# A block with two expert half-layers on one core: every other block of one stage fed as two rounded parts instead of one exact operand

## The chip, the cores and the metric

One core of a Trainium2 chip. The metric is device time in microseconds, the median of the runs shown. Engines: PE (TensorE), DVE (VectorE), ACT (ScalarE), POOL (GpSimd) and SP, which here only issues DMAs.

## The reference, cut to what matters

256 tokens of width 2048 go through an attention-and-pooling part and then through an expert layer with 16384 experts. For each token and each of 8 heads the 16 best experts are picked, and what is computed is

```
u = take(w_down, ids)                       # rows of the first expert matrix
a = gelu(einsum('cd,ced->ce', x, u)) * g    # g: the gate of each picked expert
v = take(w_up, ids)
out = einsum('ce,ced->cd', a, v)
```

Everything is float32.

## The kernel before

The kernel treats 192 tokens densely and 64 tokens sparsely. Densely means: all 16384 experts are computed for 192 tokens, in blocks of 128 experts, and a matrix of gates (zero where an expert was not picked) is multiplied onto the result. There are 128 blocks, in two halves of 64, so four stages follow each other: first expert layer of half 0, second layer of half 0, first layer of half 1, second layer of half 1. Called here down 0, up 0, down 1, up 1. Sparsely means: for the other 64 tokens the picked rows are gathered by indirect DMA and reduced on DVE, in 128 "row steps" (`sparse_step`, L1205 to L1228; 64 of the down matrix, then 64 of the up matrix) that are dealt out over the dense steps by the list `share`.

**A step** is one block. Its weights are 128 x 2048 float32, loaded by SP in two halves of 512 KB into buffers that `fill`, `take` and `give` hand out in order: five `raw` buffers, and `spare` ones where some stage has room. In down 0 the four `hi` tiles of the weight stage serve as spares, because nothing is split there. A step can use its weights in two ways:

- **exact** (all of down 0 before): PE reads the loaded buffer directly, 16 float32 matmuls of 192 columns (L354).
- **split**: ACT rounds a half block to a `hi` tile (`split_hi`, L166), DVE subtracts to get the `lo` tile (`split_lo`, L172), and PE does a pair of matmuls per 128 rows: `hi` against 384 columns (the rounded and the rest part of the activations), `lo` against 192 (`pair`, L189 and L190). The two 192-column results are added when the block is evacuated (`both_halves`: an ACT copy L194, a DVE add L195). Down 1 is done so.

**Order.** The schedule is manual: each engine's instructions stand in program order, written out by `run`. For step n it emits: the evacuation of block n-1 (`h_done`: for exact blocks an ACT gelu L1109 and an ACT copy L1111); the first 8 matmuls or pairs; one turn of the side work; the other 8; the DVE and ACT split of the second half of block n+1, if that one is split; the late DVE multiply of the evacuation (L1112); a row step, if one is due (L1213 and a POOL gather for two row steps later, L1202); another turn of the side work; and the split of the first half of block n+2, if that one is split.

**Side work in down 0** is `gate_groups`, which builds the gate matrix for 8 tokens at a time, 24 groups. A group takes three turns, so one and a half steps: eight gate matmuls on PE (L1075, called G below); then the gates go from PSUM onto what is already evacuated (DVE multiplies L1087) and into the rest (ACT copies L1089, L1090, then an ACT-issued DMA L1091), called M; then the one-hot matrices of a later group on DVE (L1056, L1059), called O. So the turns of three steps in a row are G,M / O,G / M,O. In M the ACT copies stand behind the DVE multiplies of the same tile.

Of the kernel before, what the change touches and what calls it, by code (L numbers as in the profile page):

```python
# [10 lines left out]
F32 = mybir.dt.float32  # L11
F32R = mybir.dt.float32r
U32 = mybir.dt.uint32
AF = mybir.ActivationFunctionType
# [3 lines left out]
P = 128  # L18
D = 2048
# [8 lines left out]
HB = NB // 2  # L28
SP = 64
ND = S - SP  # L30
AB = 21
RS = 24
TG = 8
HW = 1024
RAW_BUFS = 5
HL_BUFS = 4
T1_BUFS = 11
S1_BUFS = 4
KS = 9
# [54 lines left out]
def peer_block_kernel(ctx: ExitStack, tc, xT_d, c_d, cols_d, const_d, ada_d, gates_d, wide_d, blk_d, mix_d, br_d,  # L94
                      wout_d, wq_d, keys_d, down_d, up_d, rows_d, fg_d, out_d):
    nc = tc.nc
    ctx.enter_context(tc.manual_schedule())

    def ext(pool):
        return ctx.enter_context(pool)  # L100

    per = ext(tc.tile_pool(name="per", bufs=1))
    wst = ext(tc.tile_pool(name="wst", bufs=3))
# [9 lines left out]
    def psum(name):  # L113
        return psp.tile([P, 512], F32, tag="ps", name=name)
# [5 lines left out]
    spare, next_spare = [], [0]  # L120
# [23 lines left out]
    def take():  # L144
        fill()
        raw, kind = queue.popleft()
        held.append(kind)
        return raw

    def give():  # L150
        use[held.popleft()] -= 1
        fill()
# [5 lines left out]
    def split_hi(s, i):  # L158
        hw = s.w // 2
        if hw == HW:  # L160
            r = take()
        else:
            s.raw = take() if i == 0 else s.raw
            r = s.raw[:, i * hw:(i + 1) * hw]
        hi = wst.tile([P, hw], F32R, tag="hi", bufs=HL_BUFS, name="hi")
        nc.scalar.copy(hi, r)  # L166
        s.hs.append(hi)
        return r

    def split_lo(s, i, r):  # L170
        lo = wst.tile(list(r.shape), F32R, tag="lo", bufs=HL_BUFS, name="lo")
        nc.vector.tensor_sub(lo, r, s.hs[i].bitcast(F32))  # L172
        s.ls.append(lo)
        if s.w == D or i:
            give()
# [5 lines left out]
    def mm3(out, wh, wl, ah, al, start, stop):  # L181
        nc.tensor.matmul(out, wh, ah, start=start, stop=False)  # L182
        nc.tensor.matmul(out, wh, al, start=False, stop=False)  # L183
        nc.tensor.matmul(out, wl, ah, start=False, stop=stop)  # L184

    def pair(ps, wh, wl, a, start, stop):


        nc.tensor.matmul(ps[:, :2 * ND], wh, a.rearrange("p s n -> p (s n)"), start=start, stop=False)  # L189
        nc.tensor.matmul(ps[:, :ND], wl, a[:, 0, :], start=False, stop=stop)  # L190

    def both_halves(ps, out):

        nc.scalar.copy(out, ps[:, ND:2 * ND])  # L194
        nc.vector.tensor_add(out, ps[:, :ND], out)  # L195
# [10 lines left out]
    x2f = hT.rearrange("p k s -> p (k s)")[:, :KC * ND].rearrange("p (k n) -> p k n", n=ND)  # L206
# [37 lines left out]


    class Step:
        def __init__(self, src, mm, evac=None, w=D, ada=(), before=(), after=(), exact=False):
            self.exact = exact
            self.src, self.mm, self.evac, self.w = src, mm, evac, w
            self.ada, self.before, self.after = list(ada), list(before), list(after)  # L250
            self.hs, self.ls = [], []
            self.rows, self.ticks = 0, []

    steps = []
# [36 lines left out]
    def act(a):  # L291
        if a[0] == "ada":
            ada_half(a[1], a[2])
        elif a[0] == "call":
            a[1]()
        elif a[0] == "prep":
            for f in a[1].after:
                f()
        else:
            split_lo(a[1], a[2], a[3] if len(a) > 3 else split_hi(a[1], a[2]))  # L300
# [41 lines left out]
    def block_step(src, act, done, N=S, both=False, **kw):  # L342

        st = {}

        def mm(hs, ls, half):
            if half == 0:
                st["ps"] = psum("blk")
            raw = take() if kw.get("exact") else None
            for r in range(8):  # L350
                k, c = half * 8 + r, slice(r * P, (r + 1) * P)
                a = act(k)
                if raw is not None:
                    nc.tensor.matmul(st["ps"][:, :ND], raw[:, c], a, start=k == 0, stop=k == KC - 1)  # L354
                elif both:
                    pair(st["ps"], hs[half][:, c], ls[half][:, c], a, k == 0, k == KC - 1)
                else:
                    mm3(st["ps"][:, :N], hs[half][:, c], ls[half][:, c], a[:, 0, :], a[:, 1, :], k == 0, k == KC - 1)
            if raw is not None:
                give()  # L360

        return Step(src, mm, (lambda: done(st.pop("ps"))) if done else None, **kw)
# [6 lines left out]
    def tmp1(name):  # L369
        return pa.tile([P, S], F32, tag="t1", bufs=T1_BUFS, name=name)  # L370

# [324 lines left out]
    for g in range(4):  # L696
        def done(ps, g=g):
            p0 = tmp1("p0")
            nc.scalar.copy(p0, ps[:, :S])
            side2.append(pool_side(g, p0))  # L700
# [55 lines left out]
    pp = {}  # L756
# [6 lines left out]
    while gates:  # L763
        steps.append(branch_step(new.popleft() if new[0] <= have and len(new) >= len(old) else old.popleft()))
        if (len(new) + len(old)) % 2 or len(new) + len(old) < 4:
            c, g = gates.popleft()
# [250 lines left out]
    NG = ND // TG  # L1017
# [6 lines left out]
    def get_A(hs, q):  # L1024
        while len(hs["A"]) <= q:
            n = min(AB, HB - AB * len(hs["A"]))
            if n == AB:
                hs["A"].append(b16([P, NG, n, TG], F32, "A"))
            else:
                tail = hT.rearrange("p k s -> p (k s)")[:, KC * ND:KC * ND + NG * n * TG]  # L1030
                hs["A"].append(tail.rearrange("p (g n u) -> p g n u", n=n, u=TG))
        return hs["A"][q]
# [11 lines left out]
    def gate_groups():  # L1044
# [25 lines left out]
        for g in range(NG):  # L1070
# [24 lines left out]
                ohs.append(onehots(g + 2))  # L1095
            yield

    def h_done(half, bl, ps):
        hs = half_state[half]
        dst = get_A(hs, bl // AB)[:, :, bl % AB, :]  # L1100
        n = hs["g"]
        if n:
            hsum = pp["pk2"].tile([P, NG, TG], F32, tag="s1", bufs=S1_BUFS, name="hsum")
            src = hsum
            if half:
                both_halves(ps, hsum.rearrange("p g u -> p (g u)"))
            else:
                src = ps[:, :ND].rearrange("p (g u) -> p g u", u=TG)
            nc.scalar.activation(hsum, src, AF.Gelu)  # L1109
            if n < NG:  # L1110
                nc.scalar.copy(dst[:, n:], hsum[:, n:])  # L1111
            late.append(lambda: nc.vector.tensor_mul(dst[:, :n], hsum[:, :n], dst[:, :n]))  # L1112
        else:
            nc.scalar.activation(dst, ps[:, :ND].rearrange("p (g u) -> p g u", u=TG), AF.Gelu)
        hs["evac"] = bl + 1

    def room(where=None):

        spare.clear()
        if where == "h":  # L1120
            f = hT.rearrange("p k s -> p (k s)")
            spare.extend(f[:, i * HW:(i + 1) * HW] for i in range(KC * ND // HW))
        elif where:
            spare.extend(wst.tile([P, HW], F32, tag="hi", bufs=HL_BUFS, name="spare") for _ in range(HL_BUFS))

    def open_late():
        pa_ctx.close()
# [109 lines left out]
    def keep(oc):  # L1237

        pp["ctx"].close()
        pp["pf"] = ext(tc.tile_pool(name="pf", bufs=1))  # L1240
        fin["acc"] = pp["pf"].tile([P, 2, D], F32, name="acc")
        for q in range(4):
            c = slice(q * 512, (q + 1) * 512)
            evacuate(fin["acc"][:, 0, c], oc[2 * q], q)
            fold(fin["acc"][:SP, 1, c], oc[2 * q + 1])
# [26 lines left out]
    for half in range(2):  # L1272
        n0 = len(steps)
        for bl in range(HB):
            steps.append(block_step(down_d[half * HB + bl], x2act if half else lambda k: x2f[:, k, :],
                                    lambda ps, half=half, bl=bl: h_done(half, bl, ps), both=half == 1, exact=half == 0))
        if half == 0:
            for m in range(2 * KC):
                steps[n0 - 12 + m].ada.append((80 + m // 2, m % 2))
            steps[n0 + 1].ticks.append(lambda: room("split"))  # L1280
            steps[n0 + 2].ticks.append(open_late)
            steps[n0 + 5].ticks.append(lambda: side.append(gate_groups()))
            steps[n0 + 22].ticks.append(gate_row)
            steps[n0 + HB - 8].ticks.append(lambda: room())
        oc = []
        for bl in range(HB):
            steps.append(up_step(half, bl, oc))
        if half == 0:
            steps[-1].evac = lambda oc=oc: keep(oc)
# [3 lines left out]
    load_gates(n0 + 24, NA - 1, 1)  # L1293


    share = [0.95] * (HB - RS) + [0.47] * HB + [0.42] * HB + [0.55] * (HB - 4)
    total, seen = sum(share), 0.0
    for i, w in enumerate(share):
        n = int(seen / total * 2 * NP + 1e-6)
        seen += w  # L1300
        steps[n0 - 2 * HB + RS + i].rows = int(seen / total * 2 * NP + 1e-6) - n
    steps[n0 - HB + 1].ticks.append(lambda: room("h"))
    steps[n0 - 8].ticks.append(lambda: room())
    steps[n0 + 26].ticks.append(lambda: room("h"))
# [6 lines left out]
    pk, pk2 = pp["pk"], pp["pk2"]  # L1311
# [4 lines left out]
    for t in (1, 0):  # L1316
        for q in range(4):
            c = slice(q * 512, (q + 1) * 512)
            tmp = b16([P, 512], F32, "fin")
            src = oc[2 * q + t]  # L1320
            if t:
                src = fin["rows"][:, c]
# [81 lines left out]
```

## Time and profile before

| | |
|---|---|
| median of 3 runs | 2030.64 us (2026.82 to 2032.2) |
| profiled execution, its own time | 2034.78 us, of which the traced span is 2033.0 us |
| PE busy | 1977.0 us, 97% |
| DVE busy | 1662.1 us, 82% |
| ACT busy | 887.0 us, 44% |
| POOL busy | 378.5 us, 19% |
| DMA | 648.81 MB, mean 319 GB/s |

The span is longer than any busy time. The profile's chain of waits, which follows the last instruction back to what released it, runs through PE for 75% of the span, through DVE for 6%, DMA for 5%, ACT for 2%. Busy shares are means over stages of different kinds, so a stretch is read by its own rows.

### The profile page before, as it was taken

Reading aid. Unit: us, or ns where it says so; the run is one execution under the profiler, and the core shown is the slowest. Engines: PE = TensorE matmul, PEld = TensorE weight load, DVE = VectorE, ACT = ScalarE, POOL = GpSimd, SP = SyncE. Lnnn points to the kernel's source line nnn. Section 1 sums busy time; section 2 is a strip of 40 time slices with the busy share of each in tenths; the row PEclk is TensorE's granted clock in tenths of the full one; section 3 lists DMA queues with packets and bytes.
Section 4 is the critical chain, followed back from the end, with each engine's and each line's share of the span. In section 5 each row is a group of like instructions: output and inputs, shape, how many; then the busy total and the mean of one; then the engine's idle time right before and its main releaser. Section 6 shows DMA issues by size and latency. Waiting matters only on the chain.

```text
span 2033.0 us, 33021 instructions
## 1 busy us (share of the span) xinstructions
PE 1977.0 (97%) x12300; PEld 1826.7 (90%) x12300; DVE 1662.1 (82%) x2888; ACT 887.0 (44%) x1457; POOL 378.5 (19%) x384
## 2 busy tenths in 40 slices
PE   7999999999999999999999999999999999999994
PEld 5889999999999999999999888888999999888883
DVE  8787888889888978487886878888897888888886
ACT  2144554544545521012223555555555555545553
POOL 3101231102114710011111100002111112222220
PEclk8999999999999999999999999999999999999997
DMA  9996877789897788899998999998989988999992
GB/s 393 419 369 216 312 269 267 261 278 316 298 326 260 248 281 305 290 363 367 350 354 330 364 333 361 352 356 286 363 328 328 338 333 319 366 349 351 349 349 69
DMA packets 172547, 648.81 MB, mean 319 GB/s; under 512 B 21217, under 2 KB 30721, under 8 KB 155745
## 3 DMA queue, kind: packets, MB, share of 16 engines
q1 hardware_dynamic: 148144, 499.18, 68.2%
q0 software_dynamic: 19200, 136.87, 18.3%
q10 hardware_dynamic: 5042, 10.64, 1.4%
q8 instruction: 97, 1.59, 0.3%
q14 instruction: 64, 0.52, 0.1%
HBM read 636.13 MB, written 10.49 MB: 318 GB/s over the span
## 4 chain that ended last, share of the span: by engine, by line
PE 75%; DVE 6%; DMA 5%; ACT 2%; issue 2%; POOL 0%; DVEq 0%; ACTq 0%; POOLq 0%
PE blk L354 16%; PE oc L1165 12%; PE oc L1167 12%; PE blk L189 8%; PE oc L1169 6%; PE blk L183 4%; PE blk L182 4%; PE blk L184 4%; PE blk L190 4%; DMA raw<-in_blk_dram 2%; PE gps L1075 2%; DVE lo L172 2%; DMA raw<-in_down_dram 1%; DMA raw<-in_wout_dram 1%; ACT hi L166 1%
## 5 line engine op out<-in xcount | busy, mean ns | idle before, releaser
L172 DVE TENSOR_TENSOR lo<-raw,hi 128x1024 fp32r<-128x1024 f32 (+1 forms) x467 | 555.3, 1197 | 120.9 <-ACT hi L166 118.3
L166 ACT CAST hi<-raw 128x1024 fp32r<-128x1024 f32 (+1 forms) x467 | 473.3, 1020 | 387.9 <-PE oc L1165 127.1
L189 PE MATMUL blk<-xn,hi 128*128 128x384 f32 x1024 | 296.2, 363 | 2.4 <-ACT hi L166 1.7
L190 PE MATMUL blk<-xn,lo 128*128 128x192 f32 x1024 | 258.0, 252 | 1.5 <-DVE lo L172 1.5
L1202 POOL DMA_INDIRECT rows<-in_up_dram,spidx x64 | 131.6, 2055 | 494.6 <-DVE rows L1220 238.7
L354 PE MATMUL blk<-hT,raw 128*128 128x192 f32 x1280 | 212.3, 326 | 0.0
L354 PEld LDWEIGHTS blk<-hT,raw 128*128 128x128 f32 x1280 | 207.7, 190 | 0.0
L1165 PE MATMUL oc<-hi,a 128*128 128x512 f32 x512 | 202.6, 396 | 1.7 <-ACT hsum L1109 1.7
L1165 PE MATMUL oc<-lo,a 128*128 128x512 f32 x512 | 203.8, 398 | 0.0
L1167 PE MATMUL oc<-hi,a 128*128 128x512 f32 x512 | 202.7, 396 | 0.0
L1169 PE MATMUL oc<-hi,a 128*128 128x512 f32 x512 | 202.5, 395 | 0.0
L1167 PE MATMUL oc<-lo,a 128*128 128x512 f32 x512 | 201.2, 393 | 0.0
L190 PEld LDWEIGHTS blk<-xn,lo 128*128 128x128 f32 x1024 | 197.1, 193 | 2.0 <-DVE lo L172 2.0
L219 DVE SCALAR_TENSOR_TENSOR raw<-raw,cb 128x1024 f32<-128x1024 f32 x144 | 188.9, 1330 | 9.6 <-DMA raw<-in_ada_dram 7.0
L189 PEld LDWEIGHTS blk<-xn,hi 128*128 128x128 f32 x1024 | 194.0, 189 | 3.0 <-ACT hi L166 1.9
L166 ACT CAST hi<-hT 128x1024 fp32r<-128x1024 f32 x118 | 124.0, 1051 | 125.7 <-PE oc L1165 72.1
L172 DVE TENSOR_TENSOR lo<-hT,hi 128x1024 fp32r<-128x1024 f32 x118 | 142.7, 1221 | 32.6 <-ACT hi L166 32.6
L1213 DVE SCALAR_TENSOR_TENSOR rows<-rows,rows 128x2048 f32<-128x2048 f32 x64 | 146.2, 2284 | 27.9 <-DMA rows<-in_rows_dram,spidx 27.9
L1220 DVE SCALAR_TENSOR_TENSOR rows<-rows,sph,rows 128x2048 f32<-128x2048 f32 x63 | 147.7, 2344 | 1.6 <-DMA rows<-in_up_dram,spidx 1.6
L1202 POOL DMA_INDIRECT rows<-in_rows_dram,spidx x64 | 62.6, 978 | 447.0 <-DVE a L1149 233.6
L182 PE MATMUL blk<-xna,hi 128*128 128x256 f32 x480 | 138.6, 289 | 0.0
L184 PE MATMUL blk<-xna,lo 128*128 128x256 f32 x480 | 135.8, 283 | 0.0
(307 smaller groups left out, 4156.1 us busy)
## 6 DMA issues: line engine op xcount, KB each, us to landing
raw<-in_down_dram SPq DMA_DIRECT2D x181, 512.0 KB, 6.7
raw<-in_up_dram SPq DMA_DIRECT2D x165, 512.0 KB, 6.8
raw<-in_ada_dram SPq DMA_DIRECT2D x144, 512.0 KB, 5.7
hT<-in_up_dram SPq DMA_DIRECT2D x91, 512.0 KB, 7.3
raw<-in_blk_dram SPq DMA_DIRECT2D x80, 512.0 KB, 6.0
spare<-in_down_dram SPq DMA_DIRECT2D x48, 512.0 KB, 7.0
xraw<-in_ada_dram SPq DMA_DIRECT2D x36, 512.0 KB, 9.8
raw<-in_wout_dram SPq DMA_DIRECT2D x32, 512.0 KB, 5.9
```

The costliest lines, as they stand in the source:

```text
L166: nc.scalar.copy(hi, r)
L172: nc.vector.tensor_sub(lo, r, s.hs[i].bitcast(F32))
L182: nc.tensor.matmul(out, wh, ah, start=start, stop=False)
L184: nc.tensor.matmul(out, wl, ah, start=False, stop=stop)
L189: nc.tensor.matmul(ps[:, :2 * ND], wh, a.rearrange("p s n -> p (s n)"), start=start, stop=False)
L190: nc.tensor.matmul(ps[:, :ND], wl, a[:, 0, :], start=False, stop=stop)
L219: nc.vector.scalar_tensor_tensor(raw, raw, 1.0, cb[:, i * HW:(i + 1) * HW], op0=ALU.mult, op1=ALU.mult, accum_out=modp[:, i, m:m + 1])
L354: nc.tensor.matmul(st["ps"][:, :ND], raw[:, c], a, start=k == 0, stop=k == KC - 1)
L1165: nc.tensor.matmul(o, a[:, P:P + 2 * SP], w, start=st_, stop=sp_)
L1167: nc.tensor.matmul(o, a[:, :P], w, start=st_, stop=sp_)
L1169: nc.tensor.matmul(o, a[:, P + 2 * SP:], w, start=False, stop=False)
L1202: nc.gpsimd.indirect_dma_start(rows[:, j % 2, :], None, table_rows["down" if j < NP else "up"], bass.IndirectOffsetOnAxis(sp["idx"][:, j % ...
```

## The change

Down 0's blocks 26, 28, ..., 60 (18 blocks) become split blocks. Their `hi` and `lo` parts stand in two fixed tile pairs, one for each half of a block, instead of rotating tiles; two `hi` and two `lo` tiles remain as spare load buffers (before: four `hi`). The first row step moves from step 24 to step 28 (`RS`), and `share` deals the 128 row steps out anew: down 0, up 0, down 1 and up 1 get 29, 35, 29 and 35 instead of 38, 30, 26 and 34.

```diff
-RS = 24
+RS = 28
+SPLIT0 = range(26, 61, 2)
...
-        hi = wst.tile([P, hw], F32R, tag="hi", bufs=HL_BUFS, name="hi")
+        hi = pp["hi"][i] if s.fixed else wst.tile([P, hw], F32R, tag="hi", bufs=HL_BUFS, name="hi")
...
-        lo = wst.tile(list(r.shape), F32R, tag="lo", bufs=HL_BUFS, name="lo")
+        lo = pp["lo"][i] if s.fixed else wst.tile(list(r.shape), F32R, tag="lo", bufs=HL_BUFS, name="lo")
...
+    def is_split(half, bl):
+        return half == 1 or bl in SPLIT0
...
-            if half:
+            if is_split(half, bl):
                 both_halves(ps, hsum.rearrange("p g u -> p (g u)"))
...
+        elif is_split(half, bl):
+            hsum = pp["pk2"].tile([P, NG, TG], F32, tag="s1", bufs=S1_BUFS, name="hsum")
+            both_halves(ps, hsum.rearrange("p g u -> p (g u)"))
+            nc.scalar.activation(dst, hsum, AF.Gelu)
...
-            spare.extend(wst.tile([P, HW], F32, tag="hi", bufs=HL_BUFS, name="spare") for _ in range(HL_BUFS))
+            for tag in ("hi", "lo"):
+                pp[tag] = [wst.tile([P, HW], F32R, tag=tag, bufs=HL_BUFS, name=tag) for _ in range(2)]
+                spare.extend(wst.tile([P, HW], F32, tag=tag, bufs=HL_BUFS, name="spare") for _ in range(2))
...
-            steps.append(block_step(down_d[half * HB + bl], x2act if half else lambda k: x2f[:, k, :],
-                                    lambda ps, half=half, bl=bl: h_done(half, bl, ps), both=half == 1, exact=half == 0))
+            steps.append(block_step(down_d[half * HB + bl], x2act if is_split(half, bl) else lambda k: x2f[:, k, :],
+                                    lambda ps, half=half, bl=bl: h_done(half, bl, ps), both=is_split(half, bl),
+                                    exact=not is_split(half, bl), fixed=half == 0))
...
-    share = [0.95] * (HB - RS) + [0.47] * HB + [0.42] * HB + [0.55] * (HB - 4)
+    share = [0.82] * (HB - RS) + [0.55] * HB + [0.44] * HB + [0.58] * (HB - 4)
```

## Rows read from the trace of the kernel before

The columns of a stretch are: start:end, its length, then busy us of PE, PE's weight loads, DVE, ACT and POOL (instructions in brackets), granted clock, DMA share, GB/s. A timeline row is: start us, us, engine, line, instruction, and in brackets the idle time before it and what ended it.

**Rows 1.** Chain of waits, down 0: start us, us, what (x counts weight loads too).

```profile
725.54 2.60 PE blk L354 x16
...
870.32 1.78 PE gps L1075 x16
872.10 7.80 PE blk L354 x48
```

**Rows 2.** Busy time by stretch, down 0: start:end, length, busy us, clock, DMA share.

```profile
870.30:1062.00 191.70, 191.70 (x1283) 191.70 (x1282) 155.78 (x399) 41.19 (x200) 30.19 (x30) 1.00 0.97 357
```

**Rows 3.** Timeline of PE, split blocks of down 1: start, us, instruction.

```profile
1557.12 0.36 PE L189 MATMUL blk<-xn,hi 128*128 128x384 f32 x1
...
1557.41 0.36 PE L189 MATMUL blk<-xn,hi 128*128 128x384 f32 x1
```

**Rows 4.** Timeline of DVE, down 0, late: M, O, late multiply.

```profile
1062.98 0.52 DVE L1087 TENSOR_TENSOR A<-gps,A 128x84 f32<-128x84 f32 x3
1063.87 0.52 DVE L1087 TENSOR_TENSOR A<-gps,A 128x84 f32<-128x84 f32 x3 [0.37 <-PE gps L1075]
1064.31 0.68 DVE L1056 TENSOR_TENSOR o<-iota,rt 128x512 f32<-128x512 f32 x1
...
1067.56 0.33 DVE L1112 TENSOR_TENSOR A<-hsum,A 128x168 f32<-128x168 f32 x1
1067.80 2.29 DVE L1213 SCALAR_TENSOR_TENSOR rows<-rows,rows 128x2048 f32<-128x2048 f32 x1
```

**Rows 5.** Timeline of DVE, down 0, early: a row step, then M.

```profile
894.90 2.29 DVE L1213 SCALAR_TENSOR_TENSOR rows<-rows,rows 128x2048 f32<-128x2048 f32 x1 [0.34 <-DMA rows<-in_rows_dram,spidx]
...
897.12 0.59 DVE L1087 TENSOR_TENSOR A<-gps,A 128x84 f32<-128x84 f32 x4
897.63 0.68 DVE L1056 TENSOR_TENSOR o<-iota,rt 128x512 f32<-128x512 f32 x1
```

**Rows 6.** Timeline of DVE, down 1: split, add, split, multiply, split.

```profile
1419.99 0.35 DVE L195 TENSOR_TENSOR hsum<-blk,hsum 128x192 f32<-128x192 f32 x1
1420.26 1.21 DVE L172 TENSOR_TENSOR lo<-raw,hi 128x1024 fp32r<-128x1024 f32 x1
1421.39 0.35 DVE L1112 TENSOR_TENSOR A<-hsum,A 128x192 f32<-128x192 f32 x1
1421.71 1.23 DVE L172 TENSOR_TENSOR lo<-raw,hi 128x1024 fp32r<-128x1024 f32 x1
```

**Rows 7.** Timeline of ACT, down 0, early: the end of M, then an evacuation.

```profile
897.54 0.33 ACT L1089 COPY A<-gps 128x48 f32<-128x48 f32 x2 [9.92 <-DVE A L1087]
...
898.83 0.33 ACTq L1091 DMA_DIRECT2D g2d<-gst  x1
899.20 0.33 ACT L1109 ACTIVATE hsum<-blk 128x192 f32<-128x192 f32 x1 [0.40 <-PE blk L354]
899.56 0.33 ACT L1111 COPY A<-hsum 128x168 f32<-128x168 f32 x1
```

**Rows 8.** Timeline of ACT, down 1: gelu behind the DVE add, then a cast.

```profile
1420.37 0.37 ACT L1109 ACTIVATE hsum<-hsum 128x192 f32<-128x192 f32 x1 [0.94 <-DVE hsum L195]
1420.64 1.04 ACT L166 CAST hi<-raw 128x1024 fp32r<-128x1024 f32 x1
```

**Rows 9.** Timeline of ACT, down 0, late: the DMA issue that ends M.

```profile
1065.03 0.33 ACTq L1091 DMA_DIRECT2D g2d<-gst  x1
```

**Rows 10.** Waits from 870 to 1062 us: us in total, times, longest.

```profile
ACT A L1089 <- DVE A L1087: 83.5, 28, 10.3
```

**Rows 11.** Busy time by stretch: up 0, down 1, up 1, a slow stretch of down 1.

```profile
1103.00:1403.00 300.00, 298.33 (x1279) 240.06 (x1279) 242.19 (x315) 151.63 (x194) 34.10 (x31) 1.00 0.93 348
1403.00:1706.00 303.00, 299.16 (x2080) 297.99 (x2079) 257.92 (x307) 173.44 (x266) 45.25 (x27) 0.99 0.91 334
1706.00:2000.00 294.00, 294.00 (x1263) 236.99 (x1262) 248.31 (x290) 150.52 (x192) 75.62 (x32) 1.00 0.90 333
1542.00:1549.00 7.00, 6.69 (x28) 6.70 (x29) 7.00 (x10) 4.18 (x7) 1.06 (x1) 0.57 1.02 410
```

More of the change, by code (lines that the diff above doesn't have):

```diff
@@ L246, in peer_block_kernel, with __init__ @@
     class Step:
-        def __init__(self, src, mm, evac=None, w=D, ada=(), before=(), after=(), exact=False):
-            self.exact = exact
+        def __init__(self, src, mm, evac=None, w=D, ada=(), before=(), after=(), exact=False, fixed=False):
+            self.exact, self.fixed = exact, fixed
             self.src, self.mm, self.evac, self.w = src, mm, evac, w
```

## The prediction

> **What bounds the kernel now.** I read the chain of waits first, then the busy time of the stretch that is changed, then the timelines of DVE and ACT in it. The chain through down 0 is PE alone: exact blocks and G in turn [rows 1]. Between two G's lie 24 exact matmuls in 7.80 us, so a block of 16 takes 5.20; a G takes 1.78. The first G starts 144.8 us after the stage, which is block 27.5 at 5.20 plus small gaps: turn G stands between the halves of block 27, and by its number every step from 27 on is G,M (27, 30, ...), O,G (28, 31, ...) or M,O (29, 32, ...).
>
> From 870.3 to 1062 us PE is busy for all of 191.7 us, at full clock; DVE for 155.8 (81%) [rows 2]. That is five times six blocks: 38.34 us per six (6 x 5.20 + 4 x 1.78 = 38.32, so the reading fits). DMA is busy to 0.97 there but holds nothing up: no load stands in the chain. So this stage is worth what PE is worth, as long as PE is what ends last. That is what the change puts at stake, since it moves work from PE to DVE and ACT.
>
> **PE's part.** A pair for 128 rows is issued every 0.285 us (1557.12 to 1557.41) [rows 3], so a split block takes 16 x 0.285 = 4.56 us against 5.20: 0.64 saved, 11.5 us over 18 blocks, if PE never waits. Six blocks would then take 3 x 5.20 + 3 x 4.56 + 7.12 = 36.4 us.
>
> **DVE's part.** It takes its instructions in the order written, so I sum what one turn of six steps costs it, by distances from start to start where the rows allow it.
> - O: 3.25 us (1064.31 to 1067.56) [rows 4]; four in six steps, 13.0.
> - M: 0.51 early (897.12 to 897.63, four multiplies) [rows 5], and late, with six multiplies, twice 0.44 (1063.87 to 1064.31) = 0.88 [rows 4]; the 0.37 between its halves is a wait for PE that a DVE behind PE doesn't have. Four: 2.0 or 3.5.
> - the late multiply: 0.24 [rows 4]; six, 1.4.
> - a row step: 2.22 (894.90 to 897.12) [rows 5].
> - new, the `lo` of half a block: 1.13 (1420.26 to 1421.39); new, the add of a split evacuation: 0.27 [rows 6]. Six and three: 6.8 and 0.8.
>
> Without row steps that is 24.1 us early, 25.6 late. Of the new deal 26 row steps fall on steps 29 to 59, about 5.0 in six steps: 11.2 us. Together 35.3 to 36.8, as much as PE's 36.4. DVE's spare time is used up, even by its bare work.
>
> **The new waits.** DVE's `lo` needs ACT's cast, and ACT too goes in order. Three times in six steps the cast stands behind something that waits for DVE itself, and `lo` is DVE's next instruction, so DVE stands still; everything behind it (multiply, row step, O, the next `lo`) waits along, and PE for the next `lo`.
> - Step G,M with a split block (30, 36, ...): the first `lo` of block n+2 comes right after M. Step M,O with an exact block (29, 35, ...): the second `lo` of block n+1 comes right after M. ACT must first do M's copies, which wait for DVE's multiplies in the trace already (83.5 us, 28 times [rows 10]), then issue a DMA, then cast. Late: DVE is free at 1064.31, the DMA issue is at 1065.03 [rows 9], the next ACT instruction comes 0.37 after an issue (898.83 to 899.20) [rows 7], the cast takes 1.04 [rows 8], and `lo` starts 0.03 after its end (1421.68 to 1421.71 [rows 6, 8]): 1066.47, a wait of 2.16. Early: DVE free at 897.63 [rows 5], ACT free at 899.20 [rows 7], `lo` at 900.27: 2.64.
> - Step G,M with an exact block (33, 39, ...): the second `lo` comes right after the add, with only G between, and that is PE's. ACT must do the gelu that needs the add, a copy, then the cast: add at 1419.99, DVE free at 1420.26, gelu at 1420.37 [rows 6, 8]; copy 0.36 later and 0.33 long [rows 7]; cast to 1422.10, `lo` at 1422.13: 1.87.
> - The other three `lo` come after an O or a row step, which cover the cast (O,G with an exact block: 3.25 of O against 2.14).
>
> So 7.15 us of waiting early and 6.19 late. Being late does not shorten them, as each starts from DVE's own instruction. No row shows such a wait in down 0, so their bounds are zero, if something hides them, and 3 x 2.64 = 7.9. I take the worked-out values, because every link stands in a row.
>
> **The sum.** DVE is level with PE at block 29, since steps 27 and 28 carry no row step and only 3.9 and 4.6 us. From there it needs: step 29, 0.27 + 0.51 + 2.64 + 1.13 + 0.24 + 3.25 = 8.0; three early turns (steps 30 to 47) at 24.1 + 7.15 = 31.2; two late (48 to 59) at 25.6 + 6.19 = 31.7; 26 row steps, 57.7. That is 222.9 us. The last `lo` that a split block needs (the second of block 60) has 5.7 us of step 59 behind it, so it is done at 217.2, and block 60 ends half a block later, 219.5. Before, the same stretch was PE's: 5.20 + 5 x 38.34 + 6.98 (block 60 with a G) = 203.9. So block 60 ends 15.6 us later, less 1.3 for blocks 26 and 28: **14.3 us lost**. After it DVE has little to do (no O, no split) and is level again by block 63.
>
> What else moves. Nine row steps with their gathers leave down 0, 5 go to up 0, 3 to down 1, 1 to up 1. In up 0 DVE is busy 242 of 300 us [rows 11]; 5 x 2.22 makes it 253, and up 1 runs with 248 of 294 and PE busy throughout, so I take 0 there. Down 1 is closer: 258 of 303, PE idle for 3.8; three more row steps cost 0 to 6.7, I take 1. SP's loads keep their number and nine buffers, those of a split block are freed earlier, by `lo`; PE waits for no load before, the stage gets longer and nine gathers leave it: 0, with 0 to 2 us kept for the hand-over to up 0, either way. The fixed tiles make a cast wait for the matmuls of two blocks ago: long done when DVE is behind, 0, and up to half a block (2.3 us) once, before it is.
>
> By the profiled execution 2034.8 + 15.3 = 2050; it lies 4.1 above the median of the runs shown, so the forecast is **2046 us**. About 0.3% (6 us) is what a measurement of this kernel can tell from no change.
>
> **The rivals.**
> 1. *PE stays the bound* (the three waits are hidden or much shorter). DVE's bare work of 35.3 to 36.8 keeps up with 36.4, PE gains its 11.5, down 1 costs 1: 2020. For it: DVE's 81%. Against it: it leaves no room for any wait; it decides from where the waits, worked out at 36.5 us over the stage (rival 2), are under 15. The Trainium skill (Perfetto Trace Analysis, Identifying the Most-Contended Engine) has occupancy as the measure for Vector and a fair one of how close it is to its limit; by that the added 7.6 us less the row steps fit into the idle 7.2 and this rival would be the answer. The trace agrees that DVE has room now, but the rule doesn't see a wait that DVE causes itself. 0.17.
> 2. *No change.* The waits of 36.5 us in all (2.64 + 3 x 7.15 + 2 x 6.19) shrink to about 21, and the loss of 15.3 with them: 2031. For it: ACT's copies might overlap more than the rows of M show. Against it: two of the three links are single instructions with their own rows. 0.13.
> 3. *Down 1 pays too.* The three row steps there fall where DVE already ends last, 6.7 on top, 2053; with all three waits at 2.64, 3 to 5 more: 2057. For it: PE's 3.8 us of idle in down 1. Decided by whether a row step falls among its blocks 10 to 25. 0.08.
> 4. *The clock falls.* PE's new idle gaps between the halves of split blocks (up to 5 us) could bring it down, as in down 1 at 1542, where the mean of 7 us after a stall was 0.57 [rows 11]. At 1.2 GHz a block takes twice as long; an estimate from the 18 split blocks alone is 18 x 4.56 = 82, above 2110. Up 0, with 1.7 us of PE idle, keeps 1.00. The skill's rule (TensorE: Matmul & The Clock Gate, The HAM clock gate) has the throttled state as the default that activity releases; by it these gaps speak against the change. 0.02.
>
> **How the numbers follow.** The forecast has 0.60, with its own range of 2037 (the gelu wait hidden, 5 x 1.87 less) to 2054. Rivals 0.17, 0.13, 0.08, 0.02. Slower by over 0.3%: 0.60 + 0.08 + 0.02 = 0.70; within: 0.13; faster: 0.17. The range of 2025 to 2060 leaves out most of rival 1, and rival 4.
>
> **What would show it.** Right: between blocks 30 and 60 DVE stops before `lo` for ACT's cast, three times in six steps, about 2 us each, some 30 us in all; PE stops between the halves of split blocks for `lo`; split blocks still issue a pair every 0.285; DVE busy rises to about 85% and the six steps take 42 to 43 us. Wrong: PE without gaps from block 26 to 60 and a stage 11 us shorter, or DVE busy near 100% without waits for ACT.

## The result, and the profile after

| | before | after |
|---|---|---|
| median | 2030.64 us | 2048.85 us (2044.28 to 2055.03, 5 runs) |
| ratio | | 1.0078, 95% interval 1.0064 to 1.0091 |
| profiled execution | 2034.78 us | 2048.85 us, span 2047.1 us |
| DVE busy | 1662.1 us, 82% | 1710.3 us, 84% |
| down 0, first to last exact matmul | 377.3 us | 391.9 us |

The kernel is slower by 0.8% by the ratio (the two medians alone are 0.9% apart). In the profiled executions that is 14.1 us, and down 0 alone is 14.6 us longer; from the first matmul of up 0 to the end of the span it takes 0.7 us more than before (930.99 and 930.30).

Busy time by stretch, after (start:end, length, busy us of PE, its weight loads, DVE, ACT and POOL, granted clock, DMA share, GB/s): down 0 from block 27 on, a part of it, then up 0, down 1 and up 1.

```profile
868.80:1106.00 237.20, 222.16 (x1490) 217.85 (x1489) 196.54 (x472) 80.14 (x272) 30.66 (x27) 0.97 0.82 285
915.00:945.00 30.00, 27.05 (x174) 26.20 (x173) 24.36 (x54) 9.94 (x32) 3.76 (x3) 0.91 0.84 298
...
1118.00:1417.00 299.00, 295.88 (x1262) 238.02 (x1261) 253.53 (x330) 150.64 (x193) 33.72 (x36) 0.99 0.96 366
1417.00:1720.00 303.00, 301.59 (x2090) 300.41 (x2089) 262.67 (x308) 174.46 (x267) 47.17 (x28) 1.00 0.92 341
1720.00:2014.00 294.00, 294.00 (x1264) 237.02 (x1263) 253.10 (x294) 150.49 (x192) 101.17 (x34) 1.00 0.91 340
```

In down 0 PE was busy throughout [rows 2]; now it stands idle for 15 of 237 us, and DVE, at 196.5 of 237.2 (83%), isn't full either. In the three later stages PE is busy for about 99% or more, as before [rows 11]; up 0 is 3.0 us longer and down 1 2.3 us shorter. The chain of waits, close up from 950 to 970 us, says who holds the end:

```profile
951.18 1.13 DVE lo L173
952.31 0.28 DVE hsum L196
...
952.61 0.37 ACT hsum L1113
...
953.00 0.30 ACT A L1115
953.30 0.96 ACT hi L167
...
954.28 1.23 DVE lo L173
...
959.63 2.21 DVE rows L1223 x2
961.84 1.14 DVE lo L173
```

Where only PE stood [rows 1], the chain goes from DVE's add (952.31) through ACT's gelu, copy and cast back to DVE's `lo`, and then through a row step to the next `lo`. DVE's timeline there has the two kinds of wait side by side (in brackets the idle time before an instruction, and what ended it):

```profile
951.10 1.22 DVE L173 TENSOR_TENSOR lo<-raw,hi 128x1024 fp32r<-128x1024 f32 x1
952.23 0.34 DVE L196 TENSOR_TENSOR hsum<-blk,hsum 128x192 f32<-128x192 f32 x1
954.28 1.23 DVE L173 TENSOR_TENSOR lo<-spare,hi 128x1024 fp32r<-128x1024 f32 x1 [1.71 <-ACT hi L167]
...
963.16 0.23 DVE L1088 TENSOR_TENSOR A<-gps,A 128x84 f32<-128x84 f32 x1
963.99 0.54 DVE L1088 TENSOR_TENSOR A<-gps,A 128x80 f32<-128x80 f32 x3 [0.60 <-ACT A L1115]
966.98 1.22 DVE L173 TENSOR_TENSOR lo<-raw,hi 128x1024 fp32r<-128x1024 f32 x1 [2.45 <-ACT hi L167]
...
976.10 0.69 DVE L1088 TENSOR_TENSOR A<-gps,A 128x84 f32<-128x84 f32 x4
979.10 1.23 DVE L173 TENSOR_TENSOR lo<-raw,hi 128x1024 fp32r<-128x1024 f32 x1 [2.31 <-ACT hi L167]
```

and ACT's timeline shows what it did meanwhile:

```profile
952.61 0.36 ACT L1113 ACTIVATE hsum<-hsum 128x192 f32<-128x192 f32 x1 [4.31 <-DVE hsum L196]
953.00 0.30 ACT L1115 COPY A<-hsum 128x128 f32<-128x128 f32 x1
953.21 1.04 ACT L167 CAST hi<-spare 128x1024 fp32r<-128x1024 f32 x1
...
976.58 0.23 ACT L1090 COPY A<-gps 128x84 f32<-128x84 f32 x1 [9.08 <-DVE A L1088]
...
977.65 0.33 ACTq L1092 DMA_DIRECT2D g2d<-gst  x1
978.02 1.04 ACT L167 CAST hi<-raw 128x1024 fp32r<-128x1024 f32 x1 [0.40 <-ACT gst L1091]
```

At 952.23 DVE adds; ACT, idle for 4.31 us, can only then do the gelu (952.61) and the copy, and casts from 953.21 to 954.25; `lo` starts at 954.28. At 976.10 DVE multiplies; ACT, idle for 9.08, can only then copy, issue a DMA and cast to 979.06; `lo` starts at 979.10. The cast needs nothing of either; it only stands behind them in ACT's order. The waits from 855 to 1115 us (us in total, times, longest):

```profile
DVE lo L173 <- ACT hi L167: 37.4, 18, 2.6
...
PEld blk L191 <- DVE lo L173: 14.5, 13, 2.4
PE blk L191 <- DVE lo L173: 11.0, 11, 2.1
...
DVE A L1088 <- ACT A L1115: 2.8, 6, 0.6
```

Sixteen of the eighteen in the first row fall between block 29 and block 60: 33.8 us.

### The profile page after: what moved, and what is told of

It reads as the page before. It is cut to its first block, busy times and chain, and to the rows that moved or that the text cites. A ratio compares the mean times of both kernels' runs of the same rounds, so it can differ in the third digit from the quotient of the medians.

```text
span 2047.1 us, 33143 instructions
## 1 busy us (share of the span) xinstructions
PE 1977.2 (97%) x12300; PEld 1824.5 (89%) x12300; DVE 1710.3 (84%) x2942; ACT 925.9 (45%) x1511; POOL 396.5 (19%) x384
## 4 chain that ended last, share of the span: by engine, by line
PE 71%; DVE 10%; DMA 5%; ACT 3%; issue 2%; ACTq 0%; DVEq 0%; POOL 0%
PE oc L1177 12%; PE oc L1175 12%; PE blk L355 10%; PE blk L190 9%; PE oc L1179 6%; PE blk L191 4%; PE blk L184 4%; PE blk L183 4%; PE blk L185 4%; DVE lo L173 2%; DMA raw<-in_wout_dram 2%; DMA raw<-in_blk_dram 2%; ACT hi L167 1%; PE gps L1076 1%; DVE raw L220 1%
## 5 line engine op out<-in xcount | busy, mean ns | idle before, releaser
L173 DVE TENSOR_TENSOR lo<-raw,hi 128x1024 fp32r<-128x1024 f32 (+1 forms) x487 | 580.4, 1200 | 117.2 <-ACT hi L167 114.7
L167 ACT CAST hi<-raw 128x1024 fp32r<-128x1024 f32 (+1 forms) x487 | 494.3, 1021 | 380.5 <-PE oc L1175 142.1
L190 PE MATMUL blk<-xn,hi 128*128 128x384 f32 x1312 | 389.6, 368 | 4.8 <-ACT hi L167 4.1
L191 PE MATMUL blk<-xn,lo 128*128 128x192 f32 x1312 | 333.6, 254 | 11.7 <-DVE lo L173 11.7
L191 PEld LDWEIGHTS blk<-xn,lo 128*128 128x128 f32 x1312 | 253.6, 193 | 15.5 <-DVE lo L173 15.5
L190 PEld LDWEIGHTS blk<-xn,hi 128*128 128x128 f32 x1312 | 249.4, 190 | 6.0 <-ACT hi L167 4.8
L1212 POOL DMA_INDIRECT rows<-in_up_dram,spidx x64 | 150.2, 2347 | 442.5 <-DVE rows L1230 224.3
L173 DVE TENSOR_TENSOR lo<-hT,hi 128x1024 fp32r<-128x1024 f32 x118 | 143.0, 1223 | 36.2 <-ACT hi L167 36.2
L355 PE MATMUL blk<-hT,raw 128*128 128x192 f32 x960 | 160.8, 326 | 0.0
L355 PEld LDWEIGHTS blk<-hT,raw 128*128 128x128 f32 x960 | 156.1, 190 | 0.0
```

Of the source, the lines that this page charges most:

```text
L1212: nc.gpsimd.indirect_dma_start(rows[:, j % 2, :], None, table_rows["down" if j < NP else "up"], bass.IndirectOffsetOnAxis(sp["idx"][:, j % ...
```

## The experiments

The theory was that DVE's waits for casts, which DVE causes itself through ACT's order, turn PE's gain into a loss. The rivals: the fixed tiles or DVE's bare work do it (the waits only fill idle time), or the new deal of row steps, or a lower clock of PE. "Before" is the kernel before on the same chip; down 0 is the time from the first to the last start of its exact matmuls, in the profiled execution.

| kernel | median us | before | ratio (95%) | down 0, against before's 377.3 |
|---|---|---|---|---|
| after | 2048.85 | 2030.64 | 1.0078 (1.0064 to 1.0091) | +14.6 |
| first cast ahead (e3) | 2041.39 | 2033.55 | 1.0037 (1.0024 to 1.0051) | +5.7 |
| second ahead, kept (e9) | 2026.58 | 2033.45 | 0.9961 (0.9949 to 0.9974) | -1.3 |
| both ahead, kept (e8) | 2021.52 | 2033.45 | 0.9935 (0.9919 to 0.9952) | -8.7 |
| deal alone (e6) | 2031.29 | 2033.55 | 0.9992 (0.9979 to 1.0004) | +0.4 |
| every third, no wait (e4) | 2024.78 | 2033.45 | 0.9954 (0.9941 to 0.9967) | -6.8 |
| every third, a wait each (e5) | 2034.35 | 2033.45 | 1.0004 (0.999 to 1.0018) | +0.8 |
| split alone (e7) | 2075.05 | 2032.21 | 1.0198 (1.0172 to 1.0224) | +31.4 |
| both ahead, old deal (e10) | 2046.63 | 2032.21 | 1.0066 (1.0043 to 1.0089) | +12.7 |

The last column is of one execution of each kernel. Those of e9 (2032.73) and e4 (2033.7) took 6 and 9 us more than their medians, so for these two the ratio says more than the stage: e4 is 6.8 shorter in down 0 there and 5.7 longer outside of it, which was not followed up.

**Both casts ahead (e1), and the second alone (e2): two tries that tell nothing.** The cast of a first half moves ahead of the late multiply, the row step and the turn, that of a second half ahead of the evacuation. The loads are issued in the order in which the halves are now taken (that hunk is not shown).

```diff
@@ run @@
+                elif first and first[0] == "half" and first[1].fixed:
+                    parts[0][0] = first + (split_hi(first[1], first[2]),)
+                    ahead[id(first[1]), first[2]] = held.pop()
                 if steps[n - 1].evac:
...
+            for i, a in enumerate(parts[1]):
+                if a[0] == "half" and a[1].fixed:
+                    parts[1][i] = a + (split_hi(a[1], a[2]),)
             while late:
                 late.popleft()()
```

> The changed kernel, with both of ACT's casts of a split block of down 0 written earlier: the second half's ahead of the evacuation before it, the first half's ahead of the row step and of the second turn of side work. DVE's instructions and their order are the same. Theory (DVE waits for casts that stand behind its own results, 36.5 us over the stage): the waits fall under 6 us, DVE's bare work no longer ends last, PE's stage comes to its 11.5 us below the kernel before: 2020 to 2026 us. Rival (DVE's added work alone fills the stage): the work is the same, so 2044 or more. Rival (the new deal of row steps costs the time): 2044 or more.

> As e1, but only the cast of the second half of a split block is written earlier. Theory: of each six steps' three waits two go (1.7 behind the gelu, 2.2 to 2.6 behind M, and the 0.4 to 0.6 that M loses before it): about 25 us of the stage, so 2048.85 - 25 = 2024, within 5. Rivals (bare work, or the deal): 2044 or more.

They took 2052.03 us (ratio 1.0097, 1.008 to 1.0114) and 2054.59 us (1.0106, 1.0085 to 1.0126). A half that is cast ahead still needs its buffer for `lo`, but the next `take` had already handed that buffer to a later load: `lo` is made of another block's data there, and waits for that load. The waits of the first of the two:

```profile
DVE lo L176 <- DMA spare<-in_down_dram: 28.6, 5, 7.3
...
PEld blk L194 <- DVE lo L176: 20.7, 7, 6.5
```

28.6 us of a wait that the edit itself put in: neither time bears on the theory.

**The first cast alone ahead** (e3) has only the second hunk, and no buffer problem.

> As e1, but only the cast of the first half is written earlier. Theory: one wait of 2.2 to 2.6 us goes in each six steps, five in the stage, 12 us: 2037, within 4; with e2 the two add up to more than e1 gains, since e1 meets PE's own time. Rivals (bare work, or the deal): 2044 or more.

2041.39, against the ratio of after some 8 us better (0.41% of 2030.64), down 0 shorter by 8.9. On DVE the waits behind M before a first half are gone; what is left:

```profile
909.09 1.23 DVE L176 TENSOR_TENSOR lo<-raw,hi 128x1024 fp32r<-128x1024 f32 x1 [1.74 <-ACT hi L170]
...
921.74 1.23 DVE L176 TENSOR_TENSOR lo<-spare,hi 128x1024 fp32r<-128x1024 f32 x1 [2.54 <-ACT hi L170]
```

The missing ones are five of 2.11 to 2.56 in after, 11.7 us together; 8.9 of them came back. The median is 0.4 outside of what was expected.

**Both ahead, and the second alone, with the buffer kept** until its `lo` has read it (nothing is handed on while a half is held):

```diff
     def take():
-        fill()
+        if not ahead:
+            fill()
...
-    def give():
-        use[held.popleft()] -= 1
-        fill()
+    def give(key=None):
+        use[ahead.pop(key) if key in ahead else held.popleft()] -= 1
+        if not ahead:
+            fill()
```

> Both casts ahead as in e1, but no load is handed a buffer while a half that was cast ahead still stands unread in one: in e1 and e2 DVE's subtraction read a buffer that the next block's load had already been given, so that it waited for that load and the rest parts were not those of its block; their times say nothing of the theory. Theory (waits for casts behind DVE's own results): they fall under 6 us, PE ends last again, 2020 to 2027 us. Rival (DVE's bare work fills the stage by itself): 2036 or more, as e3 leaves it.

> As e8, but only the second half's cast is ahead. Theory: of the waits about 20 us (2.2 to 2.6 behind M five times, 1.7 behind the gelu five times) and 2 us inside M go, and five waits of 2.1 to 2.6 stay: 2048.85 - 22 = 2027, within 4. Rival (bare work): 2036 or more.

Both times came as expected, and the first kernel beats both the one before and the one after: 0.9935. The 2 us inside M that were expected to go with the second stayed, 3.1 in six waits in either kernel. The waits of the first (e8) between blocks 29 and 60, and its busy time there:

```profile
DVE hsum L199 <- ACT hsum L198: 10.0, 7, 1.7
...
DVE A L1098 <- ACT A L1125: 3.1, 6, 0.7
...
PEld blk L194 <- DVE lo L176: 2.8, 2, 1.6
...
DVE rows L1233 <- DMA rows<-in_rows_dram,spidx: 1.8, 2, 1.1
```
```profile
877.00:1085.00 208.00, 205.70 (x1443) 205.19 (x1442) 192.83 (x465) 80.82 (x274) 30.66 (x27) 1.00 0.90 319
```

There is no row of `lo` waiting for a cast. DVE does the same work in 208 us at 93%, and PE is busy for 99%. DVE has no free time here either: its 192.83 us of work and 15.3 of waits (10.0, 3.1, 1.8 and one of 0.4) fill the 208, so it is about level with PE, which waits for it for 2.8. The 10.0 is a remnant of the same kind: in one step of six the add waits for ACT's evacuation copy, which now stands behind M's copies and the cast put ahead of it. So the waits that DVE causes itself fell from 36.2 to some 13 us. Nothing differs from after but the place of the ACT casts and, for its sake, when buffers are handed on and the order of the loads, so the loss is shown to be those waits and what follows from them; the fixed tiles and DVE's bare work can't be it. With only the second cast ahead, the waits behind M before a first half are left:

```profile
DVE lo L176 <- ACT hi L170: 13.9, 6, 2.6
```

**The deal alone** (e6): before, with `RS` 28 and the new `share`.

> The kernel before with nothing changed but the first row step (28) and the new deal of row steps; all blocks of down 0 are exact. Theory: PE is the bound throughout and nothing it waits for has moved: 2030, within 4. Rival (the deal costs the time, in up 0 and down 1): 2040 to 2049.

No change (0.9992), and down 0 within 0.4 us. That rival falls.

**Every third block split**, 11 blocks either way, and only the turn differs:

```diff
-SPLIT0 = range(26, 61, 2)
+SPLIT0 = range(28, 61, 3)   # the other kernel: range(29, 61, 3)
```

> The changed kernel with blocks 28, 31, ..., 58 of down 0 split (11 instead of 18), nothing else changed. In these steps the first half's lo comes after O, and the second half's after a G and an exact block's evacuation, so neither cast stands behind anything that waits for DVE. Theory: no new waits; DVE needs 16.5 to 17.5 us for three steps, PE 18.5, so PE ends last and gains 11 x 0.64 = 7 us on the kernel before: 2024, within 3. Rival (bare work: 11 of 18 splits cost 11 of 18 of the 18 us): 2042.

> As e4 with blocks 29, 32, ..., 59: the same 11 splits, the same work on every engine, one step later in the turn of the side work. Now the first half's lo comes right after M each time. Theory: eleven waits of 2.1 to 2.7 us; three steps take DVE 18.9 to 19.3 us against PE's 18.5 (before: 19.2), so 2029 to 2034, 5 to 10 us above e4. Rival (bare work): the same time as e4, within 2.

Starting at 28 (e4), the first cast comes behind O and the second behind the gelu of an exact block, which doesn't wait for DVE. Starting at 29 (e5), the first comes behind M. Waits of the first, then of the second:

```profile
ACT hsum L195 <- PE blk L191: 34.8, 10, 3.9
...
DVE lo L173 <- ACT hi L167: 7.6, 4, 3.8
```
```profile
DVE lo L173 <- ACT hi L167: 25.2, 11, 2.6
...
PEld blk L191 <- DVE lo L173: 5.5, 3, 2.1
```

The first has down 0 shorter by 6.8 us, just what PE saves (11 x 0.64 = 7.0), and PE waits for no `lo`. The second has one wait per split block and loses it all again. Equal work, medians 9.6 us apart; the second is 0.35 above the time expected of it.

**The old deal**, `RS` 24 and the old `share`, with the split of after (e7), and with both casts ahead (e10):

> The changed kernel with the row steps as they were before the change: first one at step 24, and the old deal. Only the split blocks are left of the change. Theory: DVE is what ends last from block 30 to 60, so each row step there costs its full 2.2 us; the old deal has 30 of them on steps 29 to 59, the new one 26: 9 us above the changed kernel, 27 above the kernel before. Rival (PE or the clock is what ends last): the same time as the changed kernel, within 3.

> Casts ahead as in e8, with the old deal of row steps. Theory: without the waits DVE's bare work is 35 to 37 us in six steps with the new deal, beside PE's 36.4, and about 1.8 more with the old one: 37 to 39, so DVE ends last by 1 to 2 us in each of five turns: 3 to 8 us above e8, some 4 to 9 below the kernel before. If DVE had room to spare, the same as e8.

Both missed: 2075.05 where about 2059 was expected, and 14 us above before where 4 to 9 below was. Down 0 is longer than with the new deal by 16.8 and 21.4 us. The row steps from the split on, in after and in the kernel with both casts ahead and the old deal (count, shortest/median/longest ns, first and last start), the first of the latter on DVE's timeline, and the first in the kernel before:

```profile
L1223 DVE SCALAR_TENSOR_TENSOR rows<-rows,rows x27: 2280/2284/2289, 883.6 to 1102.5; 128x2048 f32<-128x2048 f32 x27
```
```profile
L1233 DVE SCALAR_TENSOR_TENSOR rows<-rows,rows x37: 2271/2282/2293, 866.0 to 1106.5; 128x2048 f32<-128x2048 f32 x37
```
```profile
865.97 2.29 DVE L1233 SCALAR_TENSOR_TENSOR rows<-rows,rows 128x2048 f32<-128x2048 f32 x1 [8.30 <-DMA rows<-in_rows_dram,spidx]
```
```profile
864.15 2.29 DVE L1213 SCALAR_TENSOR_TENSOR rows<-rows,rows 128x2048 f32<-128x2048 f32 x1 [8.21 <-DMA rows<-in_rows_dram,spidx]
```

(In after a 28th follows at 1109.35, so the difference is nine.) I had counted only the four more on steps 29 to 59. But steps 25 to 28 carry four more (by `share` the first row steps fall on steps 25 and 29, one behind `RS`; the ninth comes after step 59), and DVE's work for the first split blocks stands behind them. Eight at 2.22 each are 17.8 us, beside the 16.8 and 21.4, and neither kernel with the new deal has free time on DVE. That each costs its full time there is argued from this sum; no run shows it apart. The first also waits for its gather, 8.30 us here and 2.74 in the split alone; the kernel before has that wait too, 8.21, and there it costs nothing. How much of it DVE passes on was not tested. The span of the split alone is 41.2 us longer than before's (2074.2): 31.4 of it in down 0, 2.8 ahead of it, and 7 later, which were not followed up.

## Why the prediction was right

The forecast of 2046 stands on one reading: DVE, not PE, ends last in down 0 once blocks are split, because of waits that it causes itself. That is what the chain and the experiments show. By its steps:

- *PE saves 11.5 us if it never waits.* Split blocks issue a pair every 0.29 us in after, as in [rows 3]:

```profile
1097.98 0.36 PE L190 MATMUL blk<-xn,hi 128*128 128x384 f32 x1
...
1098.27 0.36 PE L190 MATMUL blk<-xn,hi 128*128 128x384 f32 x1
```

  With the casts ahead 8.7 of the 11.5 are there, and with every third block 6.8 of 7.0; the two pieces (5.7 and -1.3 against 14.6) make 8.9 + 15.9 = 24.8, and both together 23.3, where DVE comes level with PE (the -1.3 is of e9's long execution, so the 15.9 may be more). Rival 1 gave 2020 for this; it is the time of the kernel with both casts ahead, 2021.52.
- *A turn of six steps costs DVE 42 to 43 us.* From one M to the fourth after it, in after, with five row steps between:

```profile
1018.69 0.88 DVE L1088 TENSOR_TENSOR A<-gps,A 128x84 f32<-128x84 f32 x6
...
1061.57 0.92 DVE L1088 TENSOR_TENSOR A<-gps,A 128x84 f32<-128x84 f32 x6
```

  42.88 us; the prediction's late turn was 25.6 + 6.19 + 5 x 2.22 = 42.9.
- *The three waits.* Behind M, early 2.31 to 2.56 and late 2.08 to 2.19 (predicted 2.64 and 2.16, [rows 4 to 9]); behind the add 1.63 to 1.74 (predicted 1.87; ACT goes from the copy to the cast in 0.21 at 953.00, where I had 0.33). In all 33.8 for 36.5.
- *What was missed.* When DVE is late, the evacuation copy of ACT that M's second multiply needs is late too: six waits, 2.8 us, longest 0.6, five of them (2.4) between block 29 and block 60. It happens to fill what the others were short of: 36.2 in all.
- *Blocks 29 to 60.* 879.63 to 1098.84 us, 219.2 (predicted 219.5). Down 0 is longer by 14.6 (predicted 14.3).
- *The other stages, +1.* 0.7 measured, but by luck: the terms were 0 for up 0 and 1 for down 1. Up 0 takes 304.6 us from its first matmul to that of down 1 (before 301.6): PE waits 3.1 us for the last evacuation of down 0 (before 1.7), and the granted clock is 0.84 over the 10 us from 1124 on, which makes an estimated 1.6 us (10 x 0.16). Down 1 takes 2.3 us less. Rival 3, that down 1's row steps cost 6.7, did not come: PE is idle for 1.4 us of its 303, before for 3.8 [rows 11].
- *Rival 4, the clock.* It did give way, to a mean of 0.91 between 915 and 945 us, where PE waits for `lo`, and 0.97 over the stage, against 1.00 [rows 2]; so part of the time was at 1.2 GHz. The stage's length has no room for it, since DVE ends last there and, from block 29 to block 60, never waits for PE itself. The stretch, and all waits of DVE in it:

```profile
879.63:1098.84 219.21, 204.17 (x1362) 199.87 (x1360) 182.96 (x432) 75.28 (x252) 28.58 (x25) 0.97 0.83 288
```
```profile
DVE lo L173 <- ACT hi L167: 33.8, 16, 2.6
DVE A L1088 <- ACT A L1115: 2.4, 5, 0.6
```

  DVE's 182.96 us of work and 36.2 of waits for ACT are the 219.2. With the casts ahead the clock is 1.00, so its fall follows from the waits. The Trainium skill (TensorE: Matmul & The Clock Gate, The HAM clock gate) has the throttled state as the default that activity releases; the direction agrees with that.

The Trainium skill's measure for Vector, occupancy (Perfetto Trace Analysis, Identifying the Most-Contended Engine), reads 83% in after, less than with the casts ahead (93%), where PE waits for DVE for only 2.8 us. So the rows here go against using it alone: with the waits counted in, DVE is full in both, and the one at 83% holds PE up.

The predicted time lies 2.9 below the median. The working ended at 2050 for an execution like the profiled one, whose counterpart after took 2048.85; what is left is that before's profiled run lay 4.1 above its median and after's on it.

## What to carry to other kernels

Before work is moved to an engine with idle time, read what stands ahead of each new instruction in the order of the engine that feeds it: if something there waits for the receiving engine itself, the receiver will stand still however idle the profile shows it, and being late doesn't shorten the wait. Then the cure is order, not less work: here two casts that need nothing but a loaded buffer, put ahead of the instructions that wait, turned +0.8% into -0.65%; the buffer must then be held until its last reader. And work that costs nothing while an engine has room (nine row steps, 0) has a price once that engine is last (16.8 and 21.4 us).

## What the runs showed that was not expected

- With the casts ahead DVE kept PE fed at 93% busy (192.83 of 208.0 us) though waits fill the rest, and 8.7 of PE's 11.5 us were kept.
- The granted clock fell to a mean of 0.91 over 30 us in which PE was still busy for 27.05, and its longest wait for `lo` in the stage was 2.4.
- The first row step waits for its gather wherever it stands early: 8.21 us in the kernel before, where nothing comes of it, and 8.30 with both casts ahead and the old deal, where the first split blocks' work stands behind it.
